# Second half of the compression's first product moved behind the second queries and the gates; g's third group of products issued in sixes between the last four heads' scores

## The chip, the cores and the metric

One core of one Trainium2 chip. The metric is the device time of one execution in microseconds (us), median of the runs. Five engines work in the trace: TensorE (PE, its weight loads are listed apart as PEld), VectorE (DVE), ScalarE (ACT), GpSimd (POOL, idle here) and SyncE (SP), which issues the weight transfers.

## The reference

A two-layer model over 256 tokens of width 1024: an HGRN2 mixer, a SwiGLU, a native-sparse-attention mixer (NSA), a SwiGLU, each behind an RMS norm that is modulated by a projection of `c`. The parts that the change touches:

```python
# hgrn2_mixer: per head (8 heads, dk = dv = 128), gated linear attention
q, f, i, g = split(h @ w_in)
q = silu(q); log_f = log_sigmoid(f); k = -expm1(log_f)
G = cumsum(log_f)                       # inside a chunk
attn[t, s] = sum_k q[t,k] k[s,k] exp(G[t,k] - G[s,k])   # s <= t
o = attn @ v  (+ the carried state)
o = rms_norm(o, out_norm) * silu(g)
y = o @ w_out
# nsa_shared_kv: block compression of keys and of values
compress(t) = silu(flat_blocks(t) @ w1) @ w2     # w1: 2048 x 256
# nsa_mixer
q = rms_norm(h @ w_q[:, :1024]); gates = sigmoid(h @ w_q[:, 1024:])
o = gates0 * o_cmp + gates1 * o_sel + gates2 * o_win
```

## The kernel before

**Weights.** All weights come as one list of 1 MB entries (`schedule()`), in the order in which they are used. SP loads each entry into one of four raw buffers (`RAW = 4`). A linear entry ("lin") is split in two halves of 128x1024: ACT writes the high part `wh` (L307), DVE the low part `wl` (L308); both go to buffers of a pool of four (`wp`). The raw buffer is free when both low parts are made. Every linear product is then three matmuls (`mm3`, L484 to L486): high by high, high by low, low by high. Other entries are used as they come: "raw" entries (the compression's `w1`) and modulation entries on TensorE ("pe_ss", "pe_g", L385) keep their raw buffer until TensorE has read it.

**Order.** The code is traced in a fixed order. A scheduler that runs at compile time then gives each engine its instruction order, by the traced order as priority and by when it believes operands to be ready; so work that is traced later may fill a hole. On the chip each engine runs its list strictly in order. `tc.issue_after(ins)` adds an edge: what is traced in it on that engine comes behind `ins`.

**HGRN stage (66 to 164 us).** `ORDER["hgrn"]` is the order of steps, for pairs of heads numbered 0 to 3: `Dn` decays of pairs 2n and 2n+1 (`hgrn_decays`: ACT and DVE build for each pair the factors `X` of nine levels, 8 first and then 0 to 7, each level on the one before), `Sn` scores of pair n (`hgrn_scores`), `in` values' products of group n, `gn` the gate's products of group n (48 matmuls; groups 2 and 3 are traced behind the last `V`), `Vn` the heads' values (`hgrn_values`: products `hgpv`, an RMS norm, transposes `hgt`). Then `hgo`, the output product. A pair's scores are four blocks (two heads by two halves of the tokens): 24 small products into `psl` (levels 8 and 0 to 4), one 64-wide of level 6 and two 32-wide of level 5 into `psu`; and for each head one 128-wide product of level 7 into `psx`. In `psu` a matmul of zeros opens the block (L817) and a second one, two columns wide, closes it (L824). DVE then masks `psl` into `ab` (L827, L834), spreads it into `A` (L838) and adds `psu` (L839); ACT copies `psx` (L840).

**NSA stage (378 to 558 us).** `ORDER["nsa"]` gives steps: `c0`, `c1` the two halves of the compression's first product (`cmp`, L1105; the rest of the compression follows the second half), `q0` to `q3` the queries' products (`nq`), `G` the gates (`gates`), `n0`, `n1` query norms, `x0`, `x1` the softmax over compressed blocks, `w0`, `w1` values' products (`v`), `s`/`v` the attention's scores and values. Each half of the compression's product needs two raw entries at once and holds them until it is done. The weight list follows the same order.

The lists `hada` and `f0` say before which step of a stage a modulation entry stands.

Of the kernel before, what the change touches and what calls it, by code (L numbers as in the profile page):

```python
# [16 lines left out]
ALU = mybir.AluOpType  # L17
# [3 lines left out]
P = 128  # L21
S = 256
D = 1024
KD = 8
# [15 lines left out]
LOW = (1, 2, 4, 8, 16)  # L40
# [12 lines left out]
def _ada_g(l):  # L53
# [3 lines left out]

ORDER = {  # L60
    "hgrn": (
        "D0 i0 g0 S1 i1 S0 V0 D1 g1 S2 S3 i2 i3 V1"
    ).split(),
    "hada": [1, 1, 3, 4, 6, 7, 7, 7, 7, 7, 8, 8],
    "f0": [11, 11, 12, 12, 13, 17, 19, 20, 20, 20, 25, 25, 26, 27, 29, 30, 32, 33, 35, 36],
    "nsa": (
        "c0 q0 c1 G q1 n0 x0 s0 w0 q2 s1 q3 w1 s2 v0 v1 n1 s3 s4 a v2 v3 a a a x1 s5 a a s6 v4 v5 s7 a v6 a a "
        "a a v7 a"
    ).split(),
    "f1": [15, 16, 24, 29],  # L70
# [15 lines left out]
def schedule():  # L86
    s = []
    for k in range(KD):
        s += [("ada_ss", 0, k), ("lin", "hg_qf", k)]
    hg = [("lin", "hg_" + t[0], int(t[1:])) for t in ORDER["hgrn"] if t[0] in "ig"]  # L90
    hg += [("lin", "hg_g", n) for n in (2, 3)]
    s += _insert(hg, _ada_g(0) + _ada_ss(1), ORDER["hada"])
    f0 = [("lin", "hg_out", i) for i in range(4)]
    f0 += [("lin", "ffn_in0", i) for i in range(22)] + [("lin", "ffn_out0", i) for i in range(11)]
    s += _insert(f0, _ada_g(1) + _ada_ss("kv") + _ada_ss(2), ORDER["f0"])
    s += [("lin", "kv", i) for i in (0, 1, 2, 4)]
    a = iter(_ada_g(2) + _ada_ss(3))
    for t in ORDER["nsa"]:
        n = int(t[1:] or 0)
        if t[0] == "q":  # L100
            s.append(("lin", "nq", n))
        elif t[0] == "G":
            s.append(("half", "ng", 0))
        elif t[0] == "c":
            s += [("raw", "w1", 2 * n), ("raw", "w1", 2 * n + 1)]
        elif t[0] == "w":
            s.append(("lin", "kv", 3 + 2 * n))
        elif t[0] == "a":
            s.append(next(a))
    s += [("lin", "nsa_out", i) for i in range(4)]  # L110
    f1 = [("lin", "ffn_in1", i) for i in range(22)] + [("lin", "ffn_out1", i) for i in range(11)]
    s += _insert(f1, _ada_g(3), ORDER["f1"])
    return s


SCHED = schedule()


# [78 lines left out]
class K:  # L197
# [284 lines left out]
    def mm3(self, ps, wh, wl, hh, hl, first, last):  # L482
        mm = self.nc.tensor.matmul
        mm(ps, lhsT=wh, rhs=hh, start=first, stop=False)  # L484
        mm(ps, lhsT=wh, rhs=hl, start=False, stop=False)  # L485
        mm(ps, lhsT=wl, rhs=hh, start=False, stop=last)  # L486

    def acc_tile(self, name):
        return self.pp.tile([P, 2, 256], F32, tag="acc", bufs=3, name=name)
# [166 lines left out]
    def hgrn(self):  # L656
        nc, tp = self.nc, self.tp
        x = self.x
        self.first_stat()
        with self.tc.tile_pool(name="hg", bufs=1) as gp, self.tc.tile_pool(name="hg2", bufs=2) as g2:  # L660
            hh, hl = self.h_tiles(0)
# [14 lines left out]
            q = gp.tile([P, 8, S], F32, name="q")  # L676
            v = [gp.tile([P, 2, 512], F32, tag=f"v{i}", name=f"v{i}") for i in range(2)]

            s0 = self.hp.tile([P, KD * 258], F32, tag="hh1", name="s0")
            s1 = self.hp.tile([P, KD * 258], F32, tag="hl1", name="s1")  # L680
# [5 lines left out]
            for i in (2, 3):  # L686
                f = s0[:, 512 * (i - 2):512 * (i - 1)].rearrange("p (m s) -> p m s", m=2)
                nc.scalar.copy(f, pf[i])
                pf[i] = f
            As = {}  # L690
# [6 lines left out]
            def gate_in(n):  # L697
                ws = self.fetch("hg_g", n)
                ps = self.acc_tile(f"hg_g{n}")
                for m in range(2):  # L700
                    self.gemm(ps[:, m], self.tiles(ws[m]), hh, hl)
                return ps

            def gate_act(n, g):
                gg = g2.tile([P, 2, S], F32, tag="g", name=f"g{n}")
                self.act(gg, g, AF.Silu)
                return gg

            def gate_out(n, gg, oh, ol):
                nc.vector.tensor_tensor(gg, q[:, 2 * n:2 * n + 2], gg, op=ALU.mult)  # L710
                self.split(oh[:, 2 * n:2 * n + 2, :256], ol[:, 2 * n:2 * n + 2, :256], gg)

            Xs = {}
            for t in ORDER["hgrn"]:
                n = int(t[1:] or 0)
                if t[0] == "D":
                    Xs.update(self.hgrn_decays({m: pf[m] for m in (2 * n, 2 * n + 1)}, q, g2))
                elif t[0] == "S":
                    As[n] = self.hgrn_scores(Xs.pop(n), q[:, 2 * n:2 * n + 2], g2, n)
                elif t[0] == "i":  # L720
                    values_in(n)
                elif t[0] == "g":
                    nc.scalar.copy(graw[:, n], gate_in(n))
                elif t[0] == "V":
                    self.hgrn_values((2 * n, 2 * n + 1), As, v[n], g2, q)
            gs = [gate_act(n, graw[:, n]) for n in range(2)]
            oh, ol = self.h_tiles(1)
            for n in range(4):
                gate_out(n, gs[n] if n < 2 else gate_act(n, gate_in(n)), oh, ol)
            gate = self.need(("gate", 0))  # L730
            nxt = self.next_h(0, 1)
            for i in range(4):
                ws = self.fetch("hg_out", i)
                ps = self.acc_tile(f"hgo{i}")
# [57 lines left out]
                nc.vector.tensor_tensor(blk(X, b, 1), blk(X, b, 1), blk(qs[:, 2 * i:2 * i + 2], b, 1), op=ALU.mult)  # L792
        return Xs

    def hgrn_scores(self, X, q, g2, i):
        nc = self.nc

        psl = self.m_tile([P, 4, 112], f"psl{i}")
        psu = self.m_tile([P, 4, P], f"psu{i}")
        psx = self.m_tile([P, 2, P], f"psx{i}")  # L800
        for h in range(2):
            for tt in range(2):
                ht = h * 2 + tt
                base = tt * P
                for j in range(4):
                    s = slice(base + 32 * j, base + 32 * j + 32)
                    nc.tensor.matmul(psl[32 * j:32 * j + 32, ht, 0:32], lhsT=X[8][:, h, s], rhs=q[:, h, s],
                                     start=True, stop=True, tile_position=(0, 32 * j))
                for l, b in enumerate(LOW):
                    for j in range(4):  # L810
                        s = slice(base + 32 * j, base + 32 * j + 32)
                        r = X[l][:, h, s].rearrange("p (n two b) -> p n two b", two=2, b=b)[:, :, 1, :]
                        nc.tensor.matmul(psl[32 * j:32 * j + 32, ht, 32 + 16 * l:48 + 16 * l],
                                         lhsT=X[l][:, h, s], rhs=r, start=True, stop=True,
                                         tile_position=(0, 32 * j))
                u = psu[:, ht]
                nc.tensor.matmul(u, lhsT=self.zero, rhs=self.zero, start=True, stop=False)  # L817
                nc.tensor.matmul(u[0:64, 64:128], lhsT=X[6][:, h, base:base + 64],
                                 rhs=X[6][:, h, base + 64:base + 128], start=False, stop=False)
                for j in (0, 64):  # L820
                    nc.tensor.matmul(u[j:j + 32, j + 32:j + 64], lhsT=X[5][:, h, base + j:base + j + 32],
                                     rhs=X[5][:, h, base + j + 32:base + j + 64], start=False, stop=False,
                                     tile_position=(0, j))
                nc.tensor.matmul(u[:, 0:2], lhsT=self.zero, rhs=self.zero[:, 0:2], start=False, stop=True)  # L824
            nc.tensor.matmul(psx[:, h], lhsT=X[7][:, h, 0:P], rhs=X[7][:, h, P:2 * P], start=True, stop=True)
        ab = g2.tile([P, 4, 32], F32, tag="ab", name=f"ab{i}")
        nc.vector.tensor_tensor(ab, psl[:, :, 0:32], self.c("m_d")[:, None, :].to_broadcast([P, 4, 32]), op=ALU.mult)  # L827
        ml = self.c("m_l").rearrange("p (l j) -> p l j", l=5)
        for l, b in enumerate(LOW):
            dst = ab.rearrange("p a (n two b) -> p a n two b", two=2, b=b)[:, :, :, 1, :]  # L830
            n = 16 // b
            msk = ml[:, l].rearrange("p (n b) -> p n b", b=b)[:, None].to_broadcast([P, 4, n, b])
            src = psl[:, :, 32 + 16 * l:48 + 16 * l].rearrange("p a (n b) -> p a n b", b=b)
            nc.vector.copy_predicated(dst, msk.bitcast(U32), src)  # L834
        A = g2.tile([P, 6, P], F32, tag="A", bufs=4, name=f"A{i}")
        bm = self.c("bm4")[:, None, :, None].to_broadcast([P, 4, 4, 32])
        a4 = A[:, 0:4].rearrange("p a (j t) -> p a j t", j=4)
        nc.vector.tensor_tensor(a4, ab[:, :, None, :].to_broadcast([P, 4, 4, 32]), bm, op=ALU.mult)  # L838
        nc.vector.tensor_tensor(A[:, 0:4], A[:, 0:4], psu, op=ALU.add)  # L839
        nc.scalar.copy(A[:, 4:6], psx)  # L840
        return A

    def hgrn_values(self, ns, As, v, g2, q):

# [544 lines left out]
```

## Time and profile before

| | us |
|---|---|
| median of 3 runs | 752.18 (749.06 to 753.33) |
| profiled execution | 752.72 |
| its span | 750.9 |
| TensorE busy | 727.7 (97%) |
| VectorE busy | 569.8 (76%) |
| ScalarE busy | 397.1 (53%) |
| DMA | 174.13 MB, mean 232 GB/s |

The span is what the trace covers; 1.8 us of the execution lie outside it. Busy times are sums over instructions. Matmuls overlap in the array, so that a matmul lasts 0.28 us in a row while the next one starts 0.12 us later: what a group of matmuls costs is read from one start to the next.

### The profile page before, as it was taken

The page shows a single profiled execution, that of the slowest core. Times are in us where ns is not written, and L with a number is a line of the kernel's source. Part 1 is how long each engine was busy: PE and PEld are TensorE (multiplying, and loading weights), DVE is VectorE, ACT ScalarE, POOL GpSimd, SP SyncE. Part 2 cuts the span into 40 slices and gives each one's busy share as a digit, 9 for nine tenths or more (in the row PEclk, how much of TensorE's full clock was granted, in tenths as well). Part 3 has the DMA queues.
Part 4 walks back from the last instruction along what each step waited for, and adds up shares of the span by engine and source line. Part 5 has one row for each costly group of instructions (what it writes and reads, how often), then busy time and mean ns, then how long its engine had stood idle before and what let it go on. Part 6 is the DMA issues. An engine that isn't in the chain of part 4 may idle for free.

```text
span 750.9 us, 15924 instructions
## 1 busy us (share of the span) xinstructions
PE 727.7 (97%) x6580; PEld 667.9 (89%) x6580; DVE 569.8 (76%) x1171; ACT 397.1 (53%) x746; POOL 0.4 (0%) x5
## 2 busy tenths in 40 slices
PE   4999999999999999999999899999999999999997
PEld 2999987689999999999998798555899999999997
DVE  5995988558899898888679779678689657565641
ACT  4448856347545444544456555568666454444330
POOL 0000000000000000000000000000000000000000
PEclk9999999699999999999999999999999999999999
DMA  8998746375579897987734754463763646665700
GB/s 339 339 344 337 270 148 229 118 283 198 189 264 353 308 357 265 360 335 266 298 135 141 271 178 141 161 206 140 301 238 135 225 169 248 257 216 193 272 28 22
DMA packets 26571, 174.13 MB, mean 232 GB/s; under 512 B 3201, under 2 KB 4609, under 8 KB 6018
## 3 DMA queue, kind: packets, MB, share of 16 engines
q1 hardware_dynamic: 24912, 170.80, 62.4%
q10 hardware_dynamic: 1586, 2.32, 1.1%
q8 instruction: 51, 0.84, 0.4%
q14 instruction: 22, 0.18, 0.1%
HBM read 170.48 MB, written 1.05 MB: 228 GB/s over the span
## 4 chain that ended last, share of the span: by engine, by line
PE 88%; DVE 7%; ACT 2%; DMA 2%; issue 1%; ACTq 0%; DVEq 0%
PE ff L486 11%; PE ff L485 11%; PE ff L484 11%; PE ffo L484 6%; PE ffo L485 6%; PE ffo L486 6%; PE adapsss L385 2%; PE po L1267 2%; PE ptt L1250 2%; DVE wl L308 2%; PE s L1210 1%; PE q L485 1%; PE q L486 1%; PE nso L484 1%; PE hg_i L748 1%; PE adapsg L385 1%
## 5 line engine op out<-in xcount | busy, mean ns | idle before, releaser
L308 DVE TENSOR_TENSOR wl<-raw,wh 128x1024 fp32r<-128x1024 f32 x201 | 243.5, 1220 | 73.4 <-ACT wh L307 73.2
L307 ACT CAST wh<-raw 128x1024 fp32r<-128x1024 f32 x201 | 208.8, 1048 | 159.3 <-PE ff L485 55.3
L486 PE MATMUL ff<-hh,wl 128*128 128x256 f32 (+1 forms) x704 | 198.3, 282 | 0.0
L484 PE MATMUL ff<-hh,wh 128*128 128x256 f32 (+1 forms) x704 | 198.1, 282 | 0.0
L485 PE MATMUL ff<-hl,wh 128*128 128x256 f32 (+1 forms) x704 | 198.1, 282 | 0.0
L486 PEld LDWEIGHTS ff<-hh,wl 128*128 128x128 f32 x704 | 133.1, 189 | 0.0
L485 PEld LDWEIGHTS ff<-hl,wh 128*128 128x128 f32 x704 | 132.7, 189 | 0.3
L484 PEld LDWEIGHTS ff<-hh,wh 128*128 128x128 f32 x704 | 132.6, 189 | 0.1
L484 PE MATMUL ffo<-gh,wh 128*128 128x256 f32 x352 | 98.9, 282 | 0.6 <-DVE x L638 0.6
L485 PE MATMUL ffo<-gl,wh 128*128 128x256 f32 x352 | 98.6, 280 | 0.0
L486 PE MATMUL ffo<-gh,wl 128*128 128x256 f32 x352 | 98.5, 280 | 0.0
L359 DVE CUSTOM_DVE_ANT_0 junk<-raw,crep 128x1024 f32<-128x1024 f32 x64 | 78.0, 1219 | 4.1 <-DMA raw<-in_w 3.7
L484 PEld LDWEIGHTS ffo<-gh,wh 128*128 128x128 f32 x352 | 66.0, 188 | 1.3 <-DVE x L638 1.0
L485 PEld LDWEIGHTS ffo<-gl,wh 128*128 128x128 f32 x352 | 66.1, 188 | 0.0
L486 PEld LDWEIGHTS ffo<-gh,wl 128*128 128x128 f32 x352 | 66.1, 188 | 0.0
L479 ACT CAST gh<-fg 128x256 fp32r<-128x256 f32 x44 | 17.8, 405 | 42.0 <-DVE fg L894 41.4
L429 ACT ACTIVATE Pt<-Pt,nm 128x128 f32<-128x128 f32 x64 | 28.1, 442 | 8.9 <-DVE nm L1219 8.8
L480 DVE TENSOR_TENSOR gl<-fg,gh 128x256 fp32r<-128x256 f32 x44 | 18.5, 421 | 8.2 <-ACT gh L479 8.2
L587 ACT ACTIVATE hh<-t,mod 128x256 fp32r<-128x256 f32 x24 | 11.3, 504 | 23.6 <-DVE t L586 23.6
L385 PE MATMUL adapsss<-raw,c 128*32 128x512 f32 x128 | 21.6, 633 | 1.1 <-issue 1.1
L638 DVE SCALAR_TENSOR_TENSOR x<-ffo,mod,x 128x256 f32<-128x256 f32 x16 | 7.7, 481 | 18.5 <-PE ffo L486 18.4
L429 ACT ACTIVATE fs<-ff 128x256 f32<-128x256 f32 x38 | 14.4, 380 | 13.6 <-PE ff L486 13.6
(321 smaller groups left out, 1467.8 us busy)
## 6 DMA issues: line engine op xcount, KB each, us to landing
raw<-in_w SPq DMA_DIRECT2D x160, 1024.0 KB, 5.8
x<-in_x SPq DMA_DIRECT2D x2, 512.0 KB, 4.9
usq<-huq ACTq DMA_DIRECT2D x16, 64.0 KB, 3.0
out<-x SPq DMA_DIRECT2D x8, 128.0 KB, 1.9
cst<-in_cst ACTq DMA_DIRECT2D x1, 558.0 KB, 6.7
usk<-huk ACTq DMA_DIRECT2D x8, 64.0 KB, 2.7
raw<-in_w SPq DMA_DIRECT2D x1, 512.0 KB
rselr<-in_rsel SPq DMA_DIRECT2D x1, 256.0 KB, 2.7
```

The lines of the kernel that those rows point to most:

```text
L307: nc.scalar.copy(wh, u)
L308: nc.vector.tensor_tensor(wl, u, wh.bitcast(F32), op=ALU.subtract)
L359: nc.vector.tensor_tensor_reduce(out=junk, in0=t[:, h * D:(h + 1) * D], in1=self.crep, scale=1.0, scalar=0.0, op0=ALU.mult, op1=ALU.add, a ...
L385: nc.tensor.matmul(self.aps[32 * j:32 * j + 32, :q], lhsT=self.c32[:, k], rhs=t[:, n * D + j * q:n * D + (j + 1) * q], start=k == 0, stop= ...
L429: r = nc.scalar.activation(out, in_, func, **kw)
L479: self.nc.scalar.copy(hi, v)
L480: self.nc.vector.tensor_tensor(lo, v, hi.bitcast(F32), op=ALU.subtract)
L484: mm(ps, lhsT=wh, rhs=hh, start=first, stop=False)
L485: mm(ps, lhsT=wh, rhs=hl, start=False, stop=False)
L486: mm(ps, lhsT=wl, rhs=hh, start=False, stop=last)
L1250: nc.tensor.transpose(pt[:, e], Pt[half][:, br, e * P:(e + 1) * P], self.c("ident"))
L1267: nc.tensor.matmul(po[64 * half:64 * half + 64, t], lhsT=w[:, half], rhs=rhs, start=n == 0, stop=n == len(steps) - 1, tile_position=(0, 64 ...
```

## The change

In the HGRN stage the last two pairs' scores become steps `T2 T3` behind `i2 i3` (they were `S2 S3` ahead of them). In a `T` step, the gate's products of group 2 come as a generator (`gate_steps`): eight steps of six matmuls, each pinned behind one block of scores, and the next block of the same pair pinned behind it. The weights of that group and the modulation entries ahead of the next one are fetched in the first such step. Two modulation entries of the list move ahead of group 2 (`hada`). For all four pairs, the two matmuls of zeros of each block go away; the products into `psu` stand alone, that of level 5 at columns 64 before that at 0; and the add of `psu` on DVE is replaced by three ACT copies into `A`. In the NSA stage `c1` moves behind `q1` and `G`, with its weights.

```diff
     "hgrn": (
-        "D0 i0 g0 S1 i1 S0 V0 D1 g1 S2 S3 i2 i3 V1"
+        "D0 i0 g0 S1 i1 S0 V0 D1 g1 i2 i3 T2 T3 V1"
     ).split(),
-    "hada": [1, 1, 3, 4, 6, 7, 7, 7, 7, 7, 8, 8],
+    "hada": [1, 1, 3, 4, 6, 6, 6, 7, 7, 7, 8, 8],
...
-        "c0 q0 c1 G q1 n0 x0 s0 w0 q2 s1 q3 w1 s2 v0 v1 n1 s3 s4 a v2 v3 a a a x1 s5 a a s6 v4 v5 s7 a v6 a a "
+        "c0 q0 q1 G c1 n0 x0 s0 w0 q2 s1 q3 w1 s2 v0 v1 n1 s3 s4 a v2 v3 a a a x1 s5 a a s6 v4 v5 s7 a v6 a a "
...
+            def gate_steps(n):
+                ws = self.fetch("hg_g", n)
+                ps = gin[n] = self.acc_tile(f"hg_g{n}")
+                for e in range(8):
+                    for k in range(2 * (e % 4), 2 * (e % 4) + 2):
+                        wh, wl = self.tiles(ws[e // 4])[k]
+                        last = self.mm3(ps[:, e // 4], wh, wl, hh[:, k, :256], hl[:, k, :256], k == 0, k == KD - 1)
+                    yield last
+            between = gate_steps(2)
...
-                gate_out(n, gs[n] if n < 2 else gate_act(n, gate_in(n)), oh, ol)
+                gate_out(n, gs[n] if n < 2 else gate_act(n, gin[n] if n in gin else gate_in(n)), oh, ol)
...
-    def hgrn_scores(self, X, q, g2, i):
+    def hgrn_scores(self, X, q, g2, i, between):
...
         for h in range(2):
             for tt in range(2):
...
+                with self.tc.issue_after(prev.ins) if prev else ExitStack():
+                    last = self.head_scores(psl, psu, X, q, h, tt)
+                with self.tc.issue_after(last.ins):
+                    prev = next(between, None)
             nc.tensor.matmul(psx[:, h], lhsT=X[7][:, h, 0:P], rhs=X[7][:, h, P:2 * P], start=True, stop=True)
...
-        nc.vector.tensor_tensor(A[:, 0:4], A[:, 0:4], psu, op=ALU.add)
+        for p, n, t in ((0, 64, 64), (0, 32, 32), (64, 32, 96)):
+            nc.scalar.copy(A[p:p + n, 0:4, t:t + n], psu[p:p + n, :, t:t + n])
         nc.scalar.copy(A[:, 4:6], psx)
...
     # head_scores: the 24 products into psl as before, then
-                nc.tensor.matmul(u, lhsT=self.zero, rhs=self.zero, start=True, stop=False)
-                nc.tensor.matmul(u[0:64, 64:128], lhsT=X[6][:, h, base:base + 64],
-                                 rhs=X[6][:, h, base + 64:base + 128], start=False, stop=False)
-                for j in (0, 64):
-                    nc.tensor.matmul(u[j:j + 32, j + 32:j + 64], lhsT=X[5][:, h, base + j:base + j + 32],
-                                     rhs=X[5][:, h, base + j + 32:base + j + 64], start=False, stop=False,
-                                     tile_position=(0, j))
-                nc.tensor.matmul(u[:, 0:2], lhsT=self.zero, rhs=self.zero[:, 0:2], start=False, stop=True)
+        nc.tensor.matmul(u[0:64, 64:128], lhsT=X[6][:, h, base:base + 64],
+                         rhs=X[6][:, h, base + 64:base + 128], start=True, stop=True,
+                         tile_position=(0, 0))
+        for j in (64, 0):
+            last = nc.tensor.matmul(u[j:j + 32, j + 32:j + 64], lhsT=X[5][:, h, base + j:base + j + 32],
+                             rhs=X[5][:, h, base + j + 32:base + j + 64], start=True, stop=True,
+                             tile_position=(0, j))
+        return last
```

## Rows read from the trace of the kernel before

**Rows 1.** The page's first part: busy time, share of the span, instructions of each engine.

```profile
PE 727.7 (97%) x6580; PEld 667.9 (89%) x6580; DVE 569.8 (76%) x1171; ACT 397.1 (53%) x746; POOL 0.4 (0%) x5
```

**Rows 2.** Stretches: length, busy PE, PEld, DVE, ACT, POOL, granted clock, DMA share, GB/s.

```profile
132.00:133.00 1.00, 0.15 (x1) 0.00 (x0) 0.97 (x4) 0.00 (x0) 0.00 (x0) 0.89 0.00 0
...
146.00:147.00 1.00, 1.00 (x7) 1.00 (x8) 1.00 (x3) 0.00 (x0) 0.00 (x0) 0.78 0.26 33
...
423.00:424.00 1.00, 0.81 (x4) 0.82 (x5) 0.13 (x1) 0.00 (x0) 0.00 (x0) 0.50 1.00 406
```

**Rows 3.** List of PE's waits: total us, how many, longest us.

```profile
PE nq L486 <- DVE wl L308: 2.3, 2, 1.3
PE gates L484 <- ACT wh L307: 1.4, 1, 1.4
...
PE gates L486 <- DVE wl L308: 0.8, 1, 0.8
```

**Rows 4.** PE in order of time, one block of scores at 2.4 GHz: start, duration.

```profile
100.67 0.27 PE L807 MATMUL psl<-q,X 128*32 128x32 f32 x8
...
101.22 0.23 PE L817 MATMUL psu<-zero 128*128 128x128 bf16 x1
101.38 0.33 PE L818 MATMUL psu<-s 128*64 128x64 f32 x2
...
101.82 0.18 PE L824 MATMUL psu<-zero 128*128 128x2 bf16 x1
101.93 0.27 PE L807 MATMUL psl<-q,X 128*32 128x32 f32 x8
```

**Rows 5.** The same, one block at 1.2 GHz (first product, and that of the next).

```profile
138.96 0.33 PE L807 MATMUL psl<-q,X 128*32 128x32 f32 x8
...
140.73 0.33 PE L807 MATMUL psl<-q,X 128*32 128x32 f32 x8
```

**Rows 6.** PE in order of time: other products of the HGRN stage, first and last.

```profile
73.88 0.28 PE L484 MATMUL hg_g<-hh,wh 128*128 128x256 f32 x1
...
79.46 0.28 PE L486 MATMUL hg_g<-hh,wl 128*128 128x256 f32 x1
...
111.11 1.07 PE L385 MATMUL adapsss<-raw,c 128*32 128x512 f32 x8
...
113.05 0.39 PE L854 MATMUL hgpv<-v,A 128*128 128x128 f32 x2
...
115.65 0.36 PE L749 MATMUL hg_i<-wl,hh 128*128 128x256 f32 x1
```

**Rows 7.** PE in order of time: first block of S2, first product of hgo.

```profile
126.65 0.27 PE L807 MATMUL psl<-q,X 128*32 128x32 f32 x8
...
164.42 0.28 PE L484 MATMUL hgo<-hh,wh 128*128 128x256 f32 x1
```

**Rows 8.** DVE in order of time, then ACT: around the decays of D1.

```profile
105.12 0.29 DVE L827 TENSOR_TENSOR ab<-psl,cst 128x128 f32<-128x128 f32 x1 [1.54 <-PE psl L813]
...
106.06 0.68 DVE L839 TENSOR_TENSOR A<-A,psu 128x512 f32<-128x512 f32 x1
...
128.12 0.42 DVE L792 TENSOR_TENSOR s<-s,q 128x256 f32<-128x256 f32 x1
...
131.14 1.21 DVE L308 TENSOR_TENSOR wl<-raw,wh 128x1024 fp32r<-128x1024 f32 x1
...
145.64 1.22 DVE L308 TENSOR_TENSOR wl<-raw,wh 128x1024 fp32r<-128x1024 f32 x1
...
106.95 0.37 ACT L840 COPY A<-psx 128x256 f32<-128x256 f32 x1 [4.23 <-PE psx L825]
```

**Rows 9.** SP, then PE in order of time: weight transfers; the gates' products at 1.2 GHz.

```profile
416.68 0.83 SPq L287 DMA_DIRECT2D raw<-in_w  x2
...
423.57 0.42 PE L484 MATMUL gates<-hh,wh 128*128 128x256 f32 x1
...
426.13 0.38 PE L484 MATMUL gates<-hh,wh 128*128 128x256 f32 x1
```

More of the change, by code (lines that the diff above doesn't have):

```diff
@@ L89, in schedule @@
         s += [("ada_ss", 0, k), ("lin", "hg_qf", k)]
-    hg = [("lin", "hg_" + t[0], int(t[1:])) for t in ORDER["hgrn"] if t[0] in "ig"]
+    hg = [("lin", "hg_i" if t[0] == "i" else "hg_g", int(t[1:])) for t in ORDER["hgrn"] if t[0] in "ig"]
     hg += [("lin", "hg_g", n) for n in (2, 3)]
@@ L485, in mm3 @@
         mm(ps, lhsT=wh, rhs=hl, start=False, stop=False)
-        mm(ps, lhsT=wl, rhs=hh, start=False, stop=last)
+        return mm(ps, lhsT=wl, rhs=hh, start=False, stop=last)
     def acc_tile(self, name):
@@ L702, in gate_in @@
                 return ps
+            gin = {}
+            def gate_steps(n):
[7 more added lines that the diff above has]
+            between = gate_steps(2)
             def gate_act(n, g):
@@ L717, in hgrn @@
                     Xs.update(self.hgrn_decays({m: pf[m] for m in (2 * n, 2 * n + 1)}, q, g2))
-                elif t[0] == "S":
-                    As[n] = self.hgrn_scores(Xs.pop(n), q[:, 2 * n:2 * n + 2], g2, n)
+                elif t[0] in "ST":
+                    As[n] = self.hgrn_scores(Xs.pop(n), q[:, 2 * n:2 * n + 2], g2, n,
+                                             between if t[0] == "T" else iter(()))
                 elif t[0] == "i":
@@ L793, in hgrn_decays @@
         return Xs
-    def hgrn_scores(self, X, q, g2, i):
+    def hgrn_scores(self, X, q, g2, i, between):
         nc = self.nc
+        prev = None
         psl = self.m_tile([P, 4, 112], f"psl{i}")
@@ L802, in hgrn_scores @@
             for tt in range(2):
[L803 to L816, printed above, removed]
-                nc.tensor.matmul(u, lhsT=self.zero, rhs=self.zero, start=True, stop=False)
-                nc.tensor.matmul(u[0:64, 64:128], lhsT=X[6][:, h, base:base + 64],
-                                 rhs=X[6][:, h, base + 64:base + 128], start=False, stop=False)
-                for j in (0, 64):
-                    nc.tensor.matmul(u[j:j + 32, j + 32:j + 64], lhsT=X[5][:, h, base + j:base + j + 32],
-                                     rhs=X[5][:, h, base + j + 32:base + j + 64], start=False, stop=False,
-                                     tile_position=(0, j))
-                nc.tensor.matmul(u[:, 0:2], lhsT=self.zero, rhs=self.zero[:, 0:2], start=False, stop=True)
+                with self.tc.issue_after(prev.ins) if prev else ExitStack():
+                    last = self.head_scores(psl, psu, X, q, h, tt)
+                with self.tc.issue_after(last.ins):
+                    prev = next(between, None)
             nc.tensor.matmul(psx[:, h], lhsT=X[7][:, h, 0:P], rhs=X[7][:, h, P:2 * P], start=True, stop=True)
@@ L838, in hgrn_scores, with head_scores @@
         nc.vector.tensor_tensor(a4, ab[:, :, None, :].to_broadcast([P, 4, 4, 32]), bm, op=ALU.mult)
-        nc.vector.tensor_tensor(A[:, 0:4], A[:, 0:4], psu, op=ALU.add)
+        for p, n, t in ((0, 64, 64), (0, 32, 32), (64, 32, 96)):
+            nc.scalar.copy(A[p:p + n, 0:4, t:t + n], psu[p:p + n, :, t:t + n])
         nc.scalar.copy(A[:, 4:6], psx)
         return A
+    def head_scores(self, psl, psu, X, q, h, tt):
+        nc = self.nc
+        ht = h * 2 + tt
+        base = tt * P
+        for j in range(4):
+            s = slice(base + 32 * j, base + 32 * j + 32)
+            nc.tensor.matmul(psl[32 * j:32 * j + 32, ht, 0:32], lhsT=X[8][:, h, s], rhs=q[:, h, s],
+                             start=True, stop=True, tile_position=(0, 32 * j))
+        for l, b in enumerate(LOW):
+            for j in range(4):
+                s = slice(base + 32 * j, base + 32 * j + 32)
+                r = X[l][:, h, s].rearrange("p (n two b) -> p n two b", two=2, b=b)[:, :, 1, :]
+                nc.tensor.matmul(psl[32 * j:32 * j + 32, ht, 32 + 16 * l:48 + 16 * l],
+                                 lhsT=X[l][:, h, s], rhs=r, start=True, stop=True,
+                                 tile_position=(0, 32 * j))
+        u = psu[:, ht]
+        nc.tensor.matmul(u[0:64, 64:128], lhsT=X[6][:, h, base:base + 64],
[6 more added lines that the diff above has]
+        return last
     def hgrn_values(self, ns, As, v, g2, q):
```

## The prediction

> **What bounds the kernel now.** I read the page's busy times first: TensorE is busy 97% of the span, DVE 76%, ACT 53% [rows 1]. So a gain has to come out of TensorE's time: fewer or cheaper products, fewer waits, or products at the full clock. The list of PE's waits comes next. Of the 23 us in which PE is not busy most stand at the program's start; later ones that this change can reach are the gates' (1.4 us for a high part, 0.8 us for a low part) and one of the two waits of the queries' products (2.3 us together, the longer 1.3, so 1.0 for the other) [rows 3]. Then the granted clock by stretches, because a busy PE can be a slow one: it falls to 1.2 GHz shortly before 133 us, in a stretch where PE is busy 0.15 us of 1, and comes back between 146 and 147 us; and it stands at 0.50 again at 423 us, behind the waits of the gates [rows 2]. Last, PE in order of time in these two places. Both are what the change rearranges; nothing else of the program is touched, and the dense products behind each place show no wait on DMA or casts, so a gain made here should reach the end.
>
> **HGRN: what goes.** A block of scores at full clock takes 1.26 us from its first product to the next block's (100.67 to 101.93). In it the opening zeros hold the array 0.16 us (101.22 to 101.38), the closing ones 0.11 (101.82 to 101.93) [rows 4]. Without them a block is 0.99. There are 16 blocks, 4.3 us in all. Bounds: 0.16 a block if the closing zeros covered something that now shows, 0.49 if of the 0.44 us of levels 6 and 5 (101.38 to 101.82) half vanishes, since the level-5 product at column 64 now stands next to the level-6 one at columns 0 to 63 and could run beside it. I take 0.27, the measured one. On that point the 24 products into psl, on different columns and all 128 rows, need only 0.55 us for 48 passes [rows 4], so columns side by side do overlap. The Trainium skill, "TensorE: Matmul & The Clock Gate", Part 3, says otherwise of the loads: a weight load overlaps a running matmul only where the row group differs; by it the new order of level 5 would give nothing and a block would stay at 0.99, which is the value taken.
>
> **HGRN: what limits the scores.** The level-6 factor of S2 is made by DVE at 128.12 to 128.54 [rows 8]; S2 could not go on before, though its first product ran at 126.65 [rows 7]. That chain starts late because DVE, in its order, sits 1.54 us before a mask that waits for S0's last product into psl, until 105.12 [rows 8]. Seven blocks stand before that product, so it comes 7 x 0.27 = 1.9 us earlier, and DVE loses its adds of psu (0.68 us each, rows 8; the one in front of the chain counts). ACT gets three copies per pair instead. No row has their shapes; the nearest, the copy of psx (128x256), takes 0.37 us [rows 8], so 1.1 us per pair at most and, since ACT had stood 4.23 us before that copy, nothing at least. Against each other: level 6 at 126.3 (about 2.2 earlier), bounds 124.5 and 128.5.
>
> PE arrives there too early. Ahead of S2 it had 36 passes of modulation, where the list now leaves three entries of eight, and seven gate products that are now pinned behind the first block: 12 x 0.13 + 7 x 0.12 = 2.4 us of cover gone [rows 6], and the eight blocks of S0 and S1 are 2.2 us shorter. So it is done at about 122, runs 0.55 us of psl, and waits some 3.6 us for level 6. The change puts a wait where cover was; queued behind it on PE are all T blocks, with the gate products and psx.
>
> **HGRN: the sum from there.** Behind level 6, at full clock: eight blocks less the first psl, 7.9 - 0.5 = 7.4; gate groups 2 and 3, 96 products at (79.46 - 73.88)/47 = 0.119 = 11.4 [rows 6]; modulation, five entries of eight passes at 1.07 = 5.4; hgpv of V1, 24 passes from 113.05 to 115.65 = 2.6; psx, the transposes of o and of the modulation, 20 passes at hgpv's 0.108 = 2.2 [rows 6]. Together 29.0, so hgo at 155.3 if nothing waits. Two additions. The wait before T2 lets the clock fall as the one at 132 us did [rows 2]; I count 1.7 us, what the fall at 423 us cost the gates' products (1.4 us, below) and a little for a block at the lower clock. And behind T3 the last pair's way to hgo (masks, copies, hgpv, squares, a root of eleven small DVE steps, transposes) had nearly all of groups 2 and 3 beside it and now has group 3 alone, 48 products: I count 1.0 us, between 0 and 3. The copies stand on that way, 1.1 in place of 0.68. hgo at 158.0; before 164.42 [rows 7]. **Gain 6.4 us**, and 2 to 10 by the bounds.
>
> Group 2's weights come two list entries later, past two modulation entries on SP's queue. Their buffer is that of the last values' group, split well before T2, so they should be there in time; what it costs if their low parts are late is rival 4.
>
> **NSA.** SP could load the gates' and q1's weights only at 416.68, when the first half of cmp had been read and released its raw buffers, since the second half's entries held the other two [rows 9], and PE waited for the casts behind that. With `q1` and `G` ahead of `c1` in the list, q1 takes the buffer that c1's first entry had, loaded during the keys' products, and the gates that of the second, loaded once q0 is split. Then PE goes from the first half of cmp straight to q1 and G. Gone: 1.4 + 0.8 + 1.0 = 3.2 us of waits [rows 3]. Gone too is the low clock: 16 gate products at (426.13 - 423.57)/12 = 0.213 instead of 0.119 [rows 9], 1.4 us. The second half of cmp and the chain behind it come some 8.6 us later (5.8 of q1, 2.9 of gates by the same 0.119), beside w0 and q2; its reader, the compressed softmax, also stands behind the query norms, which come earlier with q1. I count 0.6 us given back where the chain meets the softmax. The wait of 1.3 us before q0 stays. **Gain 4.0 us**, bounds 0.5 and 4.6: DVE is full in this place with keys and hk, and three low parts (1.2 us each by that of rows 8) move into it.
>
> **Sum.** 752.7 - 6.4 - 4.0 = 742.3 against the profiled execution. That is 0.5 over the median of the runs, so 741.8: I write **742**.
>
> **Rivals.**
> 1. *The clock stays low through the T steps.* For: it lasted from 133 to 146 us over just such blocks, and the wait comes first. Against: full-width gate products now stand between them. A low block takes 140.73 - 138.96 = 1.77 [rows 5] against 1.26, so 0.5 more; eight cost 4, 48 gate products 48 x 0.094 = 4.5; 8.5 less the 1.7 counted, 749. The Trainium skill, "TensorE: Matmul & The Clock Gate", section "HAM oscillation — how this bites in real kernels", says that a wait between groups of matmuls throttles the clock and the next group runs cold; by it this rival, or the 1.7 counted, is what happens, and the two falls in this trace agree as to the fall.
> 2. *Scores bound by the decays and the tail:* level 6 stays at 128.5 and the tail costs 3. Stage gain 2.2, total 746.
> 3. *The gates' and q1's splits wait on DVE*, which is full there, and the waits move rather than go: NSA 0.5, total 745 to 746. Here the reordering doesn't do what it says. Against: cmp's first half and q1 lie between as cover.
> 4. *Slower: the pins hand g's weights to the end of the scores.* Before, a low part waited on DVE behind the decays until 131.14 [rows 8]. If that is the first half of group 2, the second T block can't start before 132.4, since the gate step pinned ahead of it waits; the second half follows 14.5 us later (the next low part then was at 145.64, rows 8), and T3's gates with it; the work behind that, at least 12 us of gates, hgpv and tail, ends at 171 to 173 instead of 164.4. Less NSA's 4.0, that is 756. It decides from about 135 us for the first half on.
>
> **How the numbers follow.** Forecast 0.50; rival 1 0.15; rival 2 0.12; rival 3 0.15; rival 4 0.08. The range runs from 736 (level 6 at 124.5, no tail, no fall, blocks at the low bound, NSA 4.6: about 6 better) to 750, over rivals 1 to 3. A measurement of this kernel tells about 0.5% (3.8 us) from no change: faster is under 748.4. Faster: the forecast, rivals 2 and 3 and a fifth of rival 1, 0.80. Same: most of rival 1 and a mild rival 4, 0.13. Slower 0.07.
>
> **What would show it.** Right: no zeros, blocks of 0.9 to 1.05 us at full clock; a wait of 2 to 5 us ahead of the first T block's level 6; hgo at 156 to 160; no wait at gates and q1, no 0.50 near that place, cmp's second half behind the gates. Wrong: a clock of 0.50 over most of T2 and T3 (rival 1), hgo later than 162 with the level-6 factor at 128 (2), waits of nq or gates on wl (3), a PE wait on a low part between T blocks (4).

## The result: slower by 1%, and the profile after

The kernel after takes 759.9 us at the median (759.5 to 761.7), the one before 752.8 in the same comparison: a ratio of 1.0097 (95% interval 1.0076 to 1.0118). The forecast was 742, with 736 to 750 as its range. The time lies outside and on the other side.

The page of the kernel after, its first part, its chain that ended last (the second of the lines), and from its DMA issues the transfers of the queries' swap (KB each, median us from issue to landing):

```profile
PE 724.3 (96%) x6548; PEld 664.5 (88%) x6548; DVE 568.4 (75%) x1167; ACT 399.0 (53%) x758; POOL 0.4 (0%) x5
...
PE 85%; DVE 7%; ACT 3%; DMA 3%; issue 1%; ACTq 0%; DVEq 0%
...
usq<-huq ACTq DMA_DIRECT2D x16, 64.0 KB, 6.6
```

TensorE is busy 3.4 us less than before [rows 1], and yet the span is 757.7 in place of 750.9, so PE idles 10.2 us more. The last line points to where: the kernel before had the same sixteen transfers, with a median of

```profile
usq<-huq ACTq DMA_DIRECT2D x16, 64.0 KB, 3.0
```

What they are stands in no part of the prediction. Behind each queries' product ACT copies the queries to `huq`; four transfers on ACT's queue swap its blocks of 32 rows into `usq` (`rotate`), and DVE multiplies `usq` by the sines (L968 after, L939 before).

**The NSA stage.** From the first of the keys' products to the first of `nso` it takes 539.6 - 386.5 = 153.1 us, before 533.0 - 390.5 = 142.4: 10.7 more. With the same 1031 products PE is busy 142.4 us in it in place of 136.5, and the other 4.8 are idle time. PE's waits there (total us, how many, longest):

```profile
PE v L765 <- DVE wl L309: 2.5, 1, 2.5
PE ptt L1279 <- DVE Pt L1265: 2.4, 1, 2.4
PE po L1296 <- ACT PT L1284: 1.6, 1, 1.6
PE nq L487 <- DVE wl L309: 1.3, 1, 1.3
```

The gates' waits and one of the two of `nq` are gone, as forecast [rows 3]. In their place stand the first three. The chain of work that ended last, from 419 to 477 us (start, duration), shows what is ahead of the first two:

```profile
420.17 0.60 ACTq L964
420.81 0.60 ACTq L964
421.45 6.84 DMA usq<-huq
428.36 0.63 issue
428.99 1.23 DVE wl L309
430.26 0.39 PE v L765
...
464.02 7.95 DMA usq<-huq
472.00 0.75 DVE usq L968
472.83 0.19 DVE Pt L1244
...
474.06 0.88 DVE Pt L1265
475.08 1.76 PE ptt L1279 x9
```

And DVE in order of time (in brackets its idle time and what ended it):

```profile
423.45 0.75 DVE L968 SCALAR_TENSOR_TENSOR usq<-usq,cols,cst 128x512 f32<-128x512 f32 x1 [4.66 <-DMA usq<-huq]
...
428.32 0.75 DVE L968 SCALAR_TENSOR_TENSOR usq<-usq,cols,cst 128x512 f32<-128x512 f32 x1 [2.86 <-DMA usq<-huq]
428.99 1.22 DVE L309 TENSOR_TENSOR wl<-raw,wh 128x1024 fp32r<-128x1024 f32 x1
```

And on ACT the high parts that the low part at 428.99 and the next one are made from:

```profile
424.22 2.00 ACT L308 CAST wh<-raw 128x1024 fp32r<-128x1024 f32 x2 [4.13 <-DMA raw<-in_w]
```

A chain gives the one releaser that came last; DVE's rows give its order, and the order tells more. The low part `wl` of the first values' weights did not need the swap at all: both high parts were there by 426.22. It only stood behind the multiply that did need it, in a list that DVE runs in order, so DVE idled 2.86 us with work in hand and PE stood until 430.26. At 472 it is the softmax steps of a head that stand behind the multiply of q3's swap.

Stretches of the kernel after (length, then busy PE, PEld, DVE, ACT, POOL, granted clock, DMA share, GB/s):

```profile
418.00:421.00 3.00, 2.67 (x19) 2.01 (x19) 0.79 (x1) 1.09 (x2) 0.00 (x0) 1.00 1.01 358
...
427.80:430.20 2.40, 0.00 (x1) 0.00 (x0) 1.88 (x3) 1.99 (x2) 0.00 (x0) 1.00 1.03 427
431.00:433.00 2.00, 2.00 (x13) 2.00 (x12) 2.00 (x3) 0.70 (x3) 0.00 (x0) 0.53 0.90 291
...
463.00:470.00 7.00, 6.41 (x32) 3.14 (x32) 6.78 (x37) 3.21 (x13) 0.00 (x0) 1.00 0.93 330
472.70:475.00 2.30, 0.02 (x3) 0.00 (x0) 2.30 (x12) 2.13 (x10) 0.00 (x0) 1.00 0.93 260
476.00:478.00 2.00, 2.00 (x10) 1.23 (x11) 2.00 (x13) 0.74 (x3) 0.00 (x0) 0.50 1.00 422
```

and one of the kernel before:

```profile
460.00:480.00 20.00, 19.41 (x152) 12.66 (x150) 16.46 (x72) 13.60 (x56) 0.00 (x0) 1.00 0.15 48
```

Two things are read here. When q1's and q3's swaps are issued, the DMA engines are full (share 1.01 and 0.93); q3's swap was issued at 458.82 before, into the stretch with 0.15. And behind PE's waits at 430 and 475 us the granted clock is 0.53 and 0.50, the lower of its two levels (1.2 GHz) nearly throughout, so each costs more than its length. The Trainium skill, "DMA: Bandwidth & Descriptors", section "Queues, rings and completion order", says that each DMA engine takes turns between the queues it has work for, a packet at a time; by that a 64 KB swap behind full queues of 1 MB loads is stretched, and the medians of 3.0 and 6.6 us agree.

**The HGRN stage.** PE's waits from 66 to 165 us, and then PE in order of time around level 6 of the first T block:

```profile
PE psu L863 <- issue: 2.3, 1, 2.3
PE psu L863 <- DVE s L808: 1.6, 1, 1.6
PE hg_g L486 <- issue: 1.4, 1, 1.4
```

```profile
122.43 0.27 PE L852 MATMUL psl<-q,X 128*32 128x32 f32 x8
...
124.61 0.30 PE L863 MATMUL psu<-s 128*64 128x64 f32 x2 [1.56 <-DVE s L808]
...
157.22 0.28 PE L485 MATMUL hgo<-hh,wh 128*128 128x256 f32 x1
...
158.46 0.65 PE L896 MATMUL hgt<-cst,o 128*128 128x128 f32 x4 [0.36 <-DVE o L893]
```

`hgo` starts at 157.22, 7.2 us ahead of [rows 7]. But its last product starts at 184.7, and before at 188.4: 3.7 us are left, and 0.9 of them belong to the start (the first `hg_g` is at 72.97, against 73.88 in [rows 6]). In between, `hgo` now holds eight transposes of the heads' values, four of the modulation and waits of 0.9 us, where it ran through before.

### The profile page after: what moved, and what is told of

Its sections match the earlier page's. It is cut to its first block, busy times and chain, and to the rows that moved or that the text cites. A ratio compares the mean times of both kernels' runs of the same rounds, so it can differ in the third digit from the quotient of the medians.

```text
span 757.7 us, 15872 instructions
## 1 busy us (share of the span) xinstructions
PE 724.3 (96%) x6548; PEld 664.5 (88%) x6548; DVE 568.4 (75%) x1167; ACT 399.0 (53%) x758; POOL 0.4 (0%) x5
## 4 chain that ended last, share of the span: by engine, by line
PE 85%; DVE 7%; ACT 3%; DMA 3%; issue 1%; ACTq 0%; DVEq 0%
PE ff L487 11%; PE ff L485 11%; PE ff L486 11%; PE ffo L485 6%; PE ffo L486 5%; PE ffo L487 5%; PE po L1296 2%; PE adapsss L386 2%; DMA usq<-huq 2%; DVE wl L309 2%; PE s L1239 1%; PE ptt L1279 1%; PE hg_i L764 1%; PE nso L485 1%; PE q L486 1%
## 5 line engine op out<-in xcount | busy, mean ns | idle before, releaser
L430 ACT ACTIVATE fs<-ff 128x256 f32<-128x256 f32 x38 | 14.4, 380 | 15.2 <-PE ff L487 15.1
L1244 DVE CUSTOM_DVE_ANT_0 Pt<-s,cst 128x128 f32<-128x128 f32 (+1 forms) x64 | 19.3, 350 | 1.4 <-PE s L1239 1.4
```

The costliest lines, as they stand in the source:

```text
L430: r = nc.scalar.activation(out, in_, func, **kw)
L1244: nc.vector.tensor_tensor_reduce(out=Pt[half][:, br, o:o + n], in0=ps[half][:, br], in1=cs[:, S - n:], scale=1.0, scalar=-3e38, op0=ALU.ad ...
```

## The experiments

The kernels of one group ran on one chip, beside the kernel before. Losses are against that: (ratio - 1) x 753 us.

**Four parts, each alone.** Is the loss that of the NSA order, or does it come from both edits meeting? `nsa_only` is the kernel before with one line changed, `hgrn_only` the kernel after with that line changed back:

```diff
-        "c0 q0 c1 G q1 n0 x0 s0 w0 ...
+        "c0 q0 q1 G c1 n0 x0 s0 w0 ...
```

> The kernel before with the NSA order alone changed (second half of the compression's first product behind q1 and the gates). Theory A, from the two traces: this part alone is what costs; between the keys' products and the output product the stage took 153.1 us in place of 142.4, so +9 to +12 us over the kernel before, with a PE wait of 2 to 3 us on a low part behind q1's rotation transfer. Theory B: the loss is one of both parts together (the HGRN part shifts the raw transfers against the NSA stage); then this part alone is within -4 to +3 us.

> The changed kernel with the NSA order of the kernel before. Theory A: -3 to -4 us against the kernel before, which is what the keys' products were earlier in the changed kernel's trace, less what its profile's start was earlier; nothing of it is given back behind. Theory B: the HGRN part's gain is lost later here too, 0 to +4 us.

`nsa_only`: 763.5, ratio 1.0148 (1.0124 to 1.0171), **+11 us** (+10.4 between the medians). `hgrn_only`: 749.1, ratio 0.9950 (0.9931 to 0.9968), **-4**. They add up to +6.3 to +7.4 (medians, ratios), and the whole change gave +7.1. So there are two separate effects, and the loss is all in the NSA order.

`zeros_only` takes the matmuls of zeros out and puts the ACT copies in, in the old order of steps. `pins_only` has the T steps and the moved list entries, and keeps zeros and DVE's add.

> The kernel before with the zero matmuls taken away and the DVE add of psu replaced by the three ACT copies, in the old order and without pins. If the zeros' 0.27 us a block all lie on the path: -4 us. If the scores of S2 and S3 are bound by the decays: -1 to -2 us. If the clock falls more without the full-width zeros: 0 to +3 us.

> The kernel before with T2, T3, the pinned gate products and the list's new order, but with the zeros and the DVE add of psu kept. If the gain of the HGRN part is the clock that no longer falls to 1.2 GHz: -3 to -5 us, with a granted clock of 1.00 from 120 to 150 us. If it is the zeros: within 1 us of the kernel before.

`zeros_only`: 749.1, ratio 0.9944 (0.9928 to 0.9961). That is all that the HGRN edits bring. `pins_only`: 758.3, ratio 1.0081 (1.0052 to 1.0109), +6. Neither expectation had that: with the zeros in place the pins cost time, without them they are worth nothing. The trace of `pins_only` shows a wait of 2.4 us for level 6 and a clock of 0.50 behind it; in the kernel after, that wait is 1.56 us and the clock stays at 1.00. No run tells how much of the 6 us that makes.

**Transfers taken away.** If the swaps' lateness is the cause, a swap without a transfer has no loss. Rival: the second half of the compression comes late and pushes the attention back. The edit, in the new NSA order (`nsa_act`), in the old one as control (`before_act`) and in the kernel after (`after_act`):

```diff
+            if name[0] == "q":
+                nc.scalar.copy(us[d:d + 32], u[e:e + 32])
+            else:
                 nc.scalar.dma_start(us[d:d + 32], u[e:e + 32])
```

> The kernel before with the new NSA order alone (c0 q0 q1 G c1), and the queries' swap of 32-row blocks for the rotation made by four ACT copies per query group in place of four 64 KB transfers on ACT's queue. Before is about 753; the new order with the transfers took 763.5 (+10.4). Theory A (the loss comes from q1's and q2's swaps landing 6 to 8 us after their issue among the 1 MB loads, with DVE standing in its order at the multiply that needs them, ahead of the low parts and of the softmax steps that PE awaits): with the transfers gone the waits of v on wl (3.3 us) and of ptt on Pt (1.7 us), and the halved clock behind each, go: 753 to 757. Theory B (the loss is the compression's second half coming 8.6 us later, which pushes the whole attention back): 761 to 765, with hidt, KC and the compressed softmax as late as in the new order with transfers. Between 757 and 761: both have a share.

> The kernel before, old NSA order, with the queries' swap made by ACT copies in place of the transfers: the control for the run above. In the old order DVE waited 2.3 us in two waits, the longer 1.2, for the queries' swap, beside other work. Theory A and B both: 751 to 754, since the transfers landed in 3.0 us there. Below 751 the transfers cost in the old order too, and what the run above gains is not all a repair of the new order; above 755 the copies themselves cost on ACT (16 copies of 32x512).

> The kernel after in full, with the queries' swap made by ACT copies in place of the transfers. The kernel after stands at 759.9; its HGRN part alone at 749.1, 4.0 below the kernel before. Theory A: the copies take away what the NSA order lost, and the sum is 749 to 753. Theory B: 757 to 761.

`nsa_act`: 753.7, ratio 1.0011 (0.9996 to 1.0025). The loss against the kernel before is gone. `before_act`: 751.8, ratio 0.9977 (0.9962 to 0.9992), so the transfers cost 1.7 us in the old order too, and some 8 to 9 us of what `nsa_act` gained repair the new order itself. `after_act`: 750.3, ratio 0.9960 (0.9947 to 0.9973). As the cause of the 10 us the rival falls on one row. The compression's transposes in the kernel before, and then in `nsa_act` (duration in ns: least, median, most; first and last start):

```profile
L1120 PE MATMUL hidt<-cst,hid x2: 270/272/273, 430.7 to 430.8; 128*128 128x128 f32 x2
```

```profile
L1123 PE MATMUL hidt<-cst,hid x2: 273/300/328, 443.5 to 443.7; 128*128 128x128 f32 x2
```

They come 12.8 us later, and the 10 us are not there. The wait of `v` on `wl` is not in the list of PE's waits of `nsa_act` any more.

What is left is not nothing. Against its own control, `before_act`, the new order is 2.0 us slower at the median, with no transfer of the queries in either, and its NSA stage takes 143.6 us in place of 140.9. The gates' waits are gone in `nsa_act`, and the clock there is 1.00, but in the attention PE has a new wait and then a stretch from 480 to 490 us with a mean clock of 0.83:

```profile
PE ptt L1253 <- ACT PT L1258: 2.3, 1, 2.3
```

```profile
480.00:490.00 10.00, 9.93 (x56) 6.13 (x56) 7.21 (x16) 3.95 (x11) 0.00 (x0) 0.83 0.00 1
```

That wait, of 2.2 to 2.3 us, stands in the three traces that have the new order with copies for q2 and q3 (`nsa_act`, `after_act`, `nsa_act23`), and not in `before_act`. Whether it comes from the copies on ACT, from the compression's lateness or from the order as such, no run separates.

**Half the move.** `gate_first` lets the second half of `cmp` pass the gates alone:

```diff
-        "c0 q0 c1 G q1 n0 ...
+        "c0 q0 G c1 q1 n0 ...
```

> The kernel before with half of the NSA move: the order c0 q0 G c1 q1, so the compression's second half passes the gates alone (2.9 us of products by the kernel before) and q1 stays behind it, the weights' list in the same order. Theory A (q1's swap among the raw loads that c1 frees is what costs): q1's swap comes as late as in the kernel before, behind the raw loads, so no such wait: 751 to 755. Theory B (lateness of the compression): 2.9 of 8.6 us of lateness, so about a third of 10.4 us: 755 to 758.

768.6, ratio 1.0198 (1.0176 to 1.0219), +15. Both theories missed it. PE's waits and the chain in its trace:

```profile
PE s L1210 <- DVE mx L1215: 4.4, 2, 3.9
PE pct L1193 <- DVE css L1190: 2.3, 2, 1.9
PE gates L484 <- ACT wh L307: 2.3, 1, 2.3
...
PE cmp L1105 <- DMA raw<-in_w: 1.6, 1, 1.6
```

```profile
413.46 3.26 PE cmp L1105 x28
416.74 4.84 DMA raw<-in_w
421.62 5.98 PE cmp L1105 x30
...
469.01 6.77 DMA usq<-huq
475.90 0.75 DVE usq L939
```

The gates alone don't cover the load of `cmp`'s second half: from 418 to 421 us PE is busy 0.56 us of 3. And a swap still lands late, at 475.8, beside loads that hold the DMA engines at a share of 0.98 from 469 to 476 us. A half-move brings waits of its own; "c1 passes less" is not "less loss". What share of the 15 us each of them has stays open.

**The order on DVE.** `nsa_defer` leaves the transfers as late as they are, and puts q1's multiply and add behind the low parts of `w0` (which is traced ahead of `n0`):

```diff
+                    with self.tc.issue_after(self.last_wl.ins):
+                        self.rot_tail()
```

> The kernel before with the new NSA order alone (763.5 so far, 10.4 over before), the queries' swap by transfers as it was, but q1's multiply that waits for its swap and the add behind it are put behind the low parts of the first values' weights (w0) on DVE; w0 is traced ahead of the query norm for that, the weights' list is the same. Theory A1 (the harm of q1's swap is DVE's fixed order: the waiting multiply holds up w0's low parts): v no longer waits 3.3 us on wl, the clock stays up there, and 4 to 6 us of the 10.4 come back: 757 to 760; the rest, at q2's swap 40 us later, stays. Theory A2 (the late swap costs through its own readers, the rotated queries and the query norm behind them): nothing comes back, 762 to 765.

761.8, ratio 1.0114 (1.0082 to 1.0146): +8.6, between the two expectations. The wait of `v` on `wl` is gone and the clock is 1.00 from 425 to 445, as the first theory said. But PE now waits elsewhere:

```profile
PE pct L1202 <- DVE css L1199: 3.2, 2, 2.2
PE s L1219 <- DVE mx L1224: 1.5, 1, 1.5
```

Those are the compressed softmax and the first scores, behind the query norm. So a better order on DVE alone brings only a part back: some 2.5 us, and by the intervals anything from 0 to 5. That the chain through the rotated queries is nearly as late as the one through the low parts would explain it, but the edit also moves `w0` ahead of `n0`, `x0` and `s0`, and no run takes the two apart. The profiled execution, at 759.05, is also the fastest of its six.

**Which swap.** `nsa_act01` has copies for q0 and q1 only, `nsa_act23` for q2 and q3 only:

> The new NSA order alone, with the swap of the first two query groups (q0, q1) made by ACT copies and that of q2 and q3 left as transfers. With all four made by ACT it took 753.7, with none 763.5. If q1's swap carries about half (its wait of 3.3 us and 1.5 to 2 us of halved clock, as the trace shows): 757 to 760. If q2's and q3's swaps, 40 us later (1.7 us of wait at ptt, and the scores behind it), carry nearly all: 761 to 764. If q1's carries all, because q2's lateness follows from it: 753 to 755.

> The new NSA order alone, with the swap of the last two query groups (q2, q3) made by ACT copies and that of q0 and q1 left as transfers: the complement of the run in which q0 and q1 had copies (5.3 over before, against 10.4 with four transfers and 0.2 to 0.8 with none). If each of the two late swaps costs its own half: 757 to 759.5, v's wait on wl of 2.5 to 3.3 us still there, and no wait of DVE on the swap near 470 us. If all of the later loss follows from q1's lateness: 761 to 764. If q2's swap carries nearly all: 753 to 755.

`nsa_act01`: 758.1, ratio 1.0067 (1.0043 to 1.0091), +5.0. `nsa_act23`: 759.5, ratio 1.0080 (1.0062 to 1.0098), +6.0, and the wait that it shares with `nsa_only` is the one of q1's place:

```profile
PE v L749 <- DVE wl L308: 2.9, 1, 2.9
```

From `nsa_only`, 6 us come back with the first pair's copies and 5 with the second's: two pairs, each with about its own half. In each pair the traces show one swap that holds DVE up ahead of a wait of PE, q1's and q3's; the runs themselves change the pair. The expectations call the later one q2's; by DVE's rows it is q3's, since q2's multiply, at 464.92, waits for nothing.

**The zeros' price.** A block was forecast at 0.99 us, and the trace has 0.87. Is the difference level 5 at column 64 beside level 6? `zeros_05` undoes the order:

```diff
-        for j in (64, 0):
+        for j in (0, 64):
```

> The kernel before with the matmuls of zeros left out and the add of psu replaced by ACT copies, as in the run at 749.1, but the two products of level 5 in their old order, columns 0 before 64. If the saving above the zeros' own 0.27 us a block comes from level 5 at column 64 starting beside level 6, which stands at columns 0 to 63: blocks of 0.95 to 1.0 us in place of 0.87, and 16 x 0.12 = 1.9 us more, 750.5 to 751.5. If it comes from the zeros (full-width passes that hold the array longer than their starts show): blocks of 0.87 and 748.5 to 749.7.

749.3, ratio 0.9949 (0.9930 to 0.9969), with blocks of 0.87. The order does nothing. What does, PE in order of time in `zeros_05` shows, from one level 6 to the next:

```profile
101.93 0.33 PE L863 MATMUL psu<-s 128*64 128x64 f32 x2
102.19 0.22 PE L867 MATMUL psu<-X 128*32 128x32 f32 x2
102.21 0.23 PE L852 MATMUL psl<-q,X 128*32 128x32 f32 x2
102.24 0.20 PE L867 MATMUL psu<-X 128*32 128x32 f32 x2
...
102.80 0.33 PE L863 MATMUL psu<-s 128*64 128x64 f32 x2
```

The next block's first `psl` products run between the two products of level 5. Before, the closing matmul of zeros over all 128 columns stood there [rows 4], and nothing passed it. So a block saves its zeros' 0.27 us and 0.12 more, and the rows put that at the closing end: from level 6 to the next block's first product it took 0.55 us before (101.38 to 101.93) and takes 0.28 here (101.93 to 102.21). Both matmuls of zeros go in every run, so that it is the closing one is read from these rows and not tested.

**Both gains together.** `zeros_act` and `zeros_05_act` (either order of level 5) have the zeros out and the swaps by copies, in the old order of steps:

> The kernel before in its old order of steps, with the matmuls of zeros left out and the add of psu replaced by three ACT copies (alone 749.1, 4.0 less than before), and with the queries' swap by ACT copies (alone 1.8 less). If the two gains lie in different stages and add up: 746.5 to 748.5. If the copies meet each other on ACT or the gain of the swap was the luck of one order: 749 to 751.

> The kernel before in its old order of steps, without the matmuls of zeros, the add of psu by three ACT copies, level 5 in its old order (blocks of 0.87 us with either order, 749.3), and the queries' swap by ACT copies. With the other order of level 5 the same kernel had a median of 746.7. If the gains add, as there: 746 to 748.5. If that median was low by chance: 749 to 751.

746.7, ratio 0.9914 (0.9884 to 0.9943), and 746.2, ratio 0.9907 (0.9889 to 0.9925). The gains of 4.2 and 1.7 add up, to 6.5 and 7.0. These beat both kernels, and by some 3.5 us also `after_act`, which has the same two gains in the new order of steps.

## Why the prediction was wrong

**The step that failed** is the NSA paragraph. Its half on the weights held: q1 and the gates start without their waits at the full clock. It then counted products and low parts that move, and not the four transfers that `rotate` issues behind q1 on ACT's queue, nor what is queued behind the multiply that waits for them. These moved from 437.8 to 419.6 us, into the loads that the freed raw buffers start. So a gain of 4.0 became a loss of 10.4 (`nsa_only`). `nsa_act` and its control show that the late swaps are 8 to 9 us of these 14.4. How much of it goes through DVE's order and how much through the rotated queries stays open after `nsa_defer`. The other 6 us are the forecast gain of 4.0 and 2.0 more: with copies in both orders the new one is still the slower, though the gates' waits are gone. The runs show a wait of 2.3 us in the attention in their place and leave its cause open. Two slips in the paragraph are small: 16 x (0.213 - 0.119) is 1.5, not 1.4, and 48 products of q1 at 0.119 are 5.7, not 5.8.

**"A gain made here should reach the end"** leaned on the products behind showing no waits before. It held the traffic of the stage fixed, while the edit changed when loads run: before 460 to 480 us had a DMA share of 0.15, after it had q3's swap among loads.

**The give-back of 0.6 us** where the compression meets the softmax can't be measured by these runs. The lateness of 12.8 us in `nsa_act` is not the 10 us, but it may have a share in the 6 that stay open.

**The zeros** were 0.27 us a block, bound 0.49; measured 0.39. The 0.99 leaned partly on the Trainium skill, "TensorE: Matmul & The Clock Gate", Part 3 (weight loads overlap a running matmul only where the row group differs). What the prediction drew from it for the order of level 5 came true: by `zeros_05` the order gives nothing. But products of all 128 rows, on other columns, run among each other here, and the measured 0.87 decides against the 0.99. Yet 16 x 0.39 = 6.2 became 4.2 in `zeros_only`: part of it went into PE's waits further on, where the clock still falls to 0.50 from 133.5 to 139 us.

**The scores' limit** was near. The first T block starts at 122.43 (forecast 122), and its wait is 1.56 us in place of 3.6, because level 6 came at the early bound of 124.5. The 1.7 us for a fall of the clock did not come: it is 1.00 through the stage. In their place came 2.3 and 1.4 us of "issue", which no step counted. That `hgo` still starts within 0.8 us of its forecast is in part luck: level 6 is 1.7 us early, and that and the missing fall stand against these 3.7. The Trainium skill, "TensorE: Matmul & The Clock Gate", section "HAM oscillation — how this bites in real kernels", lets a wait between groups of matmuls throttle the clock; the waits at 430 and 475 us agree, the one of 2.3 us at 133.3 does not (clock 1.00 behind it), while a wait of 2.5 us put down to "issue" in `zeros_only`, up to 134.26, does (0.50 around its end).

**The tail** was the mis-sized term of HGRN: hgo at 158.0 was right (157.2), and the 1.0 us was meant for all that follows. But with only group 3 between, the heads' transposes fall into `hgo` itself, which takes 27.5 us from its first to its last product in place of 24.0: 3.5 more, where 1.0 was counted. Its end is 2.8 us earlier once the start's 0.9 is taken off, not 6.4. So HGRN brought 4.0 us by `hgrn_only`, not 6.4, and `zeros_only`, with the same 4.0, shows that the pins bring nothing.

**The rivals.** Rival 3 named the place, low parts that wait on DVE, but as waits that move, at no loss; it stopped at DVE's load and did not ask what its queue waits for. Rival 4, the one on the slower side, looked for it among the T blocks, where no PE wait on a low part stands. The chance of 0.07 for slower was that of the wrong mechanism.

## What to carry to other kernels

List every transfer that a moved step issues, and what stands on each engine's queue behind the first reader of it: a small transfer that cost 1.7 us where it stood is late among large loads, and an engine that runs its list in order hands the lateness to work that does not need it. Where such a transfer only shuffles a few rows, copies on an engine with time to spare take it out of that traffic; look then for new waits on that engine. And give an edit's control the same repair: against the kernel before, the repaired order looked free, against the repaired kernel before it was not. Two edits that share no stage should be run apart first; here one of them was worth 4 us and hid under the other's 11.

## What was not expected of the hardware

By the rows of one block, a matmul of zeros two columns wide costs more than its 0.11 us: the next block's products, on other columns, started only behind it. Without both matmuls of zeros a block is 0.39 us shorter, 0.12 more than the two held.

PE's waits put down to "issue" in the scores, of 0.9 to 2.5 us, stand close to a 16 KB packet on the instruction queue. In the kernel after, in the stretch from 132 to 134 us (packets, MB, share of 16 engines' time):

```profile
q8 instruction: 1, 0.02, 3.0%
```

That packet starts at 133.14 and takes 0.96 us, and PE's wait of 2.3 us starts at 133.34; the one of 1.4 us at 140.41 starts while a packet runs that starts at 139.45. In the kernel before and in the experiments' traces such packets start within 1.5 us of these waits too. But others pass without such a wait, as the one at 142.98 us here. That the engine waits for its own instructions there fits, but no run tested it.
